# A hybrid decoder block on one core: the products that normalise x are pinned behind the second slot's logits

## The chip, the core and the metric

The kernel runs on one core of a Trainium2 chip. The metric is the device time of one execution in microseconds (us). The core has a matrix engine (TensorE, PE in the rows), three engines for elementwise work (VectorE or DVE, ScalarE or ACT, GpSimd or POOL) and a queue engine that issues DMAs (SyncE, SP). Each of them takes its own instructions one after another and waits, where needed, until another engine or a DMA has got far enough.

## The reference

One layer on 512 tokens of width 1024, float32 throughout:

```python
h = rms_norm(x, g_mix)
z = h @ w_in                     # q, k, v of mixers A and C, branch B, three gates
o_a = dilated window attention   # 12 heads in 3 groups (window, dilation): (128,1) (512,4) (2048,16);
                                 # head j of the groups ("slot j") is merged by softmax over their log-sum-exp
o_b = rg_lru_branch(...)         # conv, gated linear recurrence, GeLU gate
o_c = moba_attention(...)        # 8 heads, own block and one earlier block of 256 keys
x = x + (gt_0*(o_a @ p_a) + gt_1*(o_b @ p_b) + gt_2*(o_c @ p_c)) @ w_out
x = x + (silu(gate) * up) @ w_down       # [gate, up] = rms_norm(x, g_ffn) @ w_gu
return rms_norm(x, g_final)
```

## The kernel before, in words

**Products.** Every matrix product is taken as three products of split operands, hi*hi + hi*lo + lo*hi (`mm3`, lines 200 to 202). The weights come as 147 chunks of 128x1024, in the order of one list. For each chunk `stage` issues the DMA to `wraw` (three buffers), ScalarE casts it to `whi` (line 178) and VectorE or, for chunks 7 to 61, GpSimd subtracts to get `wlo` (line 183, four pieces of 256 columns). A `project` is 24 products with 512 columns each. Results go to the eight PSUM banks (`bank`), so a new product can have to wait for the readers of an old one.

**Two forms of x.** `X` is the split of x*g (`xhi`, `xlo`), without the normalisation; what is projected from it is multiplied by the row of 1/rms afterwards (`unscaled`, line 479: `qt`, `kt`, from `rq` and `rb`). `XN` is the split of x*g*rb. To make it the kernel loads x once more (`reload`, eight tiles `xt2`, shown as `xt` in the rows), multiplies (line 926, VectorE), casts `hi` (line 249, ScalarE) and subtracts to get `lo` (line 250, VectorE).

**Mixer A, slot by slot.** For slot j, `la(j)` gives three steps of logits: `s0` (line 562, `head_logits`), `s1` and `s2` (lines 579 and 585, `class_logits`: add the bias, then add and take the minimum into `m` or `stp`). `wa(j)` takes exponentials (line 594), adds their sums (line 710) and exchanges the statistics through DRAM, `exch` (lines 718 and 720), since groups are laid out by token or by residue class. `wa2(j)` computes the factors from `mm` (line 728) to `ff` and scales the probabilities (line 599). `ta(j)` transposes them on TensorE (lines 608 and 622, the flips) and splits them into `ph`, `pl` (lines 611, 612) and `pp` (lines 628, 629). `xa(j)` multiplies these with the values (lines 659 and 780).

**Order.** Code is written in the order of the list below, with some steps woven into a projection. The framework's scheduler then sets the order on each engine by its own estimate of times, not by the order in the code alone. `tc.keep_in_program_order` keeps an instruction behind everything that is written earlier for its engine. The stretch of interest, as written (`fa(h, i, w)` projects pair i of half h, w = 0 for q and 1 for k):

```python
reload(); d0, st = la(0)
for outs in weave(class_values_g(), 32, st, 12): VA.append(values_out(outs, True))
wa(d0); fa(0, 2, 0); fa(0, 2, 1); wa2(d0)
renorm(range(8))
d1, st = la(1)
VC.append(values_out(values_mm(st, 12)))
wa(d1); st = ta(d0)
VC.append(values_out(values_mm(st)))
fa(1, 0, 0); xa(d0); fa(1, 0, 1); wa2(d1); fa(1, 1, 0)   # and so on
```

Of the kernel before, what the change touches and what calls it, by code (L numbers as in the profile page):

```python
# [10 lines left out]
ALU = mybir.AluOpType  # L11
# [7 lines left out]
KT = 8  # L19
# [112 lines left out]
def layer_kernel(tc, x0p, xT, wts, tab, oneh, msk, idn, gfin, out):  # L132
    nc = tc.nc
# [3 lines left out]
    with (  # L137
# [10 lines left out]
        def uid(s):  # L148
            cnt[0] += 1
            return f"{s}_{cnt[0]}"  # L150
# [7 lines left out]
        def f32(ap):  # L158
            return ap.bitcast(F32)
# [69 lines left out]
        def project(act, kind="m", steps=(), first=0):  # L229
            return weave(project_g(act, kind), 8, steps, first)  # L230
# [36 lines left out]
        prm = cst.tile([128, 48], F32)  # L267
# [4 lines left out]
        for k in range(KT):  # L272
            if k == 0:
                xt = xp[:, 0:512]
            else:
                xt = tp.tile([128, 512], F32, name=uid("xt"), tag="bias")
                nc.sync.dma_start(xt, xT[k])
            for p in FIRST[k]:
# [7 lines left out]
                lo, in0=xt, scalar=g, in1=f32(hi), op0=ALU.mult, op1=ALU.subtract  # L286
# [305 lines left out]
        def expo(lay, negm, den):  # L592
            for qb in range(4):
                nc.scalar.activation(lay[qb][0], lay[qb][0], AF.Exp, scale=-1.0,
                                     bias=negm[:, qb : qb + 1], accum_out=den[:, qb : qb + 1])
# [22 lines left out]
        def flip_pairs(srcs):  # L618

            bt = bank()  # L620
            for i, p in enumerate(srcs):
                nc.tensor.transpose(bt[:, i * 128 : i * 128 + 128], p, ident)  # L622
            r = []
            for b in range(2):
                t = slot(F32R, "pp")
                t4 = t.rearrange("p (c two n) -> p c two n", two=2, n=128)
                src = bt[:, b * 256 : b * 256 + 256].rearrange("p (c n) -> p c n", c=2)
                nc.scalar.copy(t4[:, :, 0, :], src)
                nc.vector.tensor_sub(t4[:, :, 1, :], src, f32(t4[:, :, 0, :]))
                r.append(t)  # L630
            return r
# [36 lines left out]
        def ea(ps, half, i, w, scaled=False):  # L668
            pair = A_PAIRS[half][i]
            perm = [g > 0 for g, _ in pair]  # L670
            r = None if scaled else (rq, rb)[w]
            t = (q_tiles, k_tiles)[w](ps, r, perm)
            for n in range(2):
                qk[pair[n] + (w,)] = t[n]

        def fa(half, i, w, steps=(), first=0):
            scaled = half == 1
            ea(project(XN if scaled else X, "ma", steps, first), half, i, w, scaled)

        def st_part(st, s, o):  # L680

            c = o * 8 + s * 4
            return st[:, c : c + 4]
# [19 lines left out]
        def wa(d):  # L703

            stn, stp, j = d["stn"], d["stp"], d["j"]
            expo(d["lay"][0], st_part(stn, 0, 0), st_part(stn, 1, 0))
            dd = sm.tile([128, 8], F32, name=uid("dd"), tag="dd")
            for g in (1, 2):
                expo(d["lay"][g], st_part(stp, 0, 0), dd[:, g * 4 - 4 : g * 4])
            nc.vector.tensor_add(st_part(stp, 1, 0), dd[:, 0:4], dd[:, 4:8])  # L710
            a = exch[j : j + 1, :]

            def dram(n, by):
                ap = [[1, 128], [512, 2], [128, 4]] if by == 0 else [[4, 128], [512, 2], [1, 4]]
                return bass.AP(tensor=a.tensor, offset=a.offset + n * 1024, ap=ap)

            for n, st in enumerate((stn, stp)):
                nc.scalar.dma_start(dram(n, n), st[:, 0:8])
            for n, st in enumerate((stp, stn)):
                nc.sync.dma_start(st[:, 8:16], dram(n, 1 - n))  # L720
# [26 lines left out]
        def ta(d):  # L747
            j = d["j"]

            def vf(kt):  # L750
                return VA[0][kt][:, j * 128 : j * 128 + 128]

            d["m0"], steps = turn(d["lay"][0], vf, True)
            d["p"] = {}

            def cls(g):
                d["p"][g] = flip_pairs([p for p, _ in d["lay"][g]])

            return steps + [lambda g=g: cls(g) for g in (1, 2)]
# [155 lines left out]
        x_again = []  # L915
# [4 lines left out]
                nc.sync.dma_start(xt, xT[k])  # L920
                x_again.append(xt)

        def renorm(ks):
            for k in ks:
                xt = x_again[k]
                nc.vector.scalar_tensor_tensor(xt, in0=xt, scalar=prm[:, k : k + 1], in1=rb,
                                               op0=ALU.mult, op1=ALU.mult)
                XN.append(split(xt))

        zs = []  # L930
# [19 lines left out]
        rb = norm_all(dg)  # L950
# [10 lines left out]
        for outs in weave(class_values_g(), 32, st, 12):  # L961
# [2 lines left out]
        fa(0, 2, 0)  # L964
        fa(0, 2, 1)
        wa2(d0)
        renorm(range(8))
        d1, st = la(1)
        VC.append(values_out(values_mm(st, 12)))
        wa(d1)  # L970
        st = ta(d0)
        VC.append(values_out(values_mm(st)))
        fa(1, 0, 0)
# [27 lines left out]
                                op0=ALU.mult)  # L1001
# [83 lines left out]
        for m in range(8):  # L1085
# [7 lines left out]
            for b in (0, 2, 1):  # L1093
                ps = bank()
                nk = len(O[b])
                for k in range(nk):
# [6 lines left out]
                                               op0=ALU.add, op1=ALU.mult)  # L1103
# [12 lines left out]
        for m in range(8):  # L1116
            xr = tp.tile([128, 512], F32, name=uid("xr"), tag="bias")
            nc.sync.dma_start(xr, xT[m])
            if m == 0:
# [10 lines left out]
                                           op0=ALU.mult, op1=ALU.subtract)  # L1130
# [68 lines left out]
        for tb in range(4):  # L1199
# [4 lines left out]
            for c0, c1 in cuts:  # L1204
# [18 lines left out]
                if (c0, c1) != cuts[-1]:  # L1223
# [4 lines left out]
                                            op0=ALU.mult, op1=ALU.add)  # L1228
# [113 lines left out]
```

## Time and profile before

| what | value |
|---|---|
| median of 3 runs (lowest to highest) | 889.67 us (889.59 to 889.92) |
| the profiled execution, its span | 888.6 us, 886.6 us |
| TensorE, VectorE, ScalarE, GpSimd busy | 875.2, 472.8, 399.3, 283.9 us |
| granted TensorE clock over the span | 0.996 |

The span is the time from the first to the last instruction of the profiled execution; some 2 us lie around it. Times in the rows count from the start of the span. Shares of busy time tell how much an engine had to do, not whether anyone waited for it: that is read from the waits and from the order in time.

### The profile page before, as it was taken

Reading aid. Unit: us, or ns where it says so; the run is one execution under the profiler, and the core shown is the slowest. Engines: PE = TensorE matmul, PEld = TensorE weight load, DVE = VectorE, ACT = ScalarE, POOL = GpSimd, SP = SyncE. Lnnn points to the kernel's source line nnn. Section 1 sums busy time; section 2 is a strip of 40 time slices with the busy share of each in tenths; the row PEclk is TensorE's granted clock in tenths of the full one; section 3 lists DMA queues with packets and bytes.
Section 4 is the critical chain, followed back from the end, with each engine's and each line's share of the span. In section 5 each row is a group of like instructions: output and inputs, shape, how many; then the busy total and the mean of one; then the engine's idle time right before and its main releaser. Section 6 shows DMA issues by size and latency. Waiting matters only on the chain.

```text
span 886.6 us, 11269 instructions
## 1 busy us (share of the span) xinstructions
PE 875.2 (99%) x4166; PEld 737.4 (83%) x4166; DVE 472.8 (53%) x922; ACT 399.3 (45%) x692; POOL 283.9 (32%) x328
## 2 busy tenths in 40 slices
PE   9999999999999999999999999999999999999996
PEld 7897988888888888888888888888888888888885
DVE  7498947566665656647425445444444444322226
ACT  7376754664675567762323434333223332222213
POOL 2157364655543434675111312111222111000004
PEclk9999999999999999999999999999999999999999
DMA  7247332652322221232223322222222222222202
GB/s 276 93 158 111 94 127 88 108 133 96 95 95 84 84 95 47 97 119 95 95 95 119 119 92 84 88 94 95 95 95 99 100 103 104 96 95 95 95 24 96
DMA packets 40279, 90.28 MB, mean 102 GB/s; under 512 B 13988, under 2 KB 15780, under 8 KB 40224
## 3 DMA queue, kind: packets, MB, share of 16 engines
q1 hardware_dynamic: 34048, 88.26, 30.8%
q10 hardware_dynamic: 5824, 0.98, 0.7%
q8 instruction: 33, 0.54, 0.3%
q0 software_dynamic: 352, 0.33, 0.2%
q14 instruction: 22, 0.18, 0.1%
HBM read 87.34 MB, written 2.20 MB: 101 GB/s over the span
## 4 chain that ended last, share of the span: by engine, by line
PE 88%; DVE 4%; issue 3%; POOL 2%; DMA 2%; ACT 1%; DVEq 0%; POOLq 0%; ACTq 0%
PE ps L200 23%; PE ps L201 23%; PE ps L202 23%; PE ps L1189 12%; POOL wlo L183 2%; DMA wraw<-in_wts 2%; PE ps L659 2%; PE ps L608 1%; PE ps L555 1%; PE ps L554 1%; DVE y L1234 1%; DVE lo L250 0%; PE ps L622 0%; PE ps L780 0%; ACT junk L1220 0%
## 5 line engine op out<-in xcount | busy, mean ns | idle before, releaser
L178 ACT CAST whi<-wraw 128x1024 fp32r<-128x1024 f32 (+1 forms) x149 | 154.6, 1039 | 274.9 <-issue 101.5
L183 POOL TENSOR_TENSOR wlo<-wraw,whi 128x256 fp32r<-128x256 f32 x220 | 169.6, 803 | 181.1 <-ACT whi L178 181.0
L200 PE MATMUL ps<-hi,whi 128*128 128x512 f32 x520 | 205.2, 395 | 0.0
L201 PE MATMUL ps<-lo,whi 128*128 128x512 f32 x520 | 202.9, 390 | 0.0
L202 PE MATMUL ps<-hi,wlo 128*128 128x512 f32 x520 | 202.7, 390 | 0.0
L183 DVE TENSOR_TENSOR wlo<-wraw,whi 128x1024 fp32r<-128x1024 f32 (+1 forms) x94 | 117.5, 1250 | 115.5 <-ACT whi L178 115.5
L200 PE MATMUL ps<-uhi,whi 128*128 128x512 f32 x352 | 137.9, 392 | 0.0
L202 PE MATMUL ps<-uhi,wlo 128*128 128x512 f32 x352 | 137.1, 389 | 0.0
L201 PE MATMUL ps<-ulo,whi 128*128 128x512 f32 x352 | 136.9, 389 | 0.0
L202 PEld LDWEIGHTS ps<-hi,wlo 128*128 128x128 f32 x520 | 97.6, 188 | 20.6
L200 PEld LDWEIGHTS ps<-hi,whi 128*128 128x128 f32 x520 | 97.7, 188 | 18.8
L201 PEld LDWEIGHTS ps<-lo,whi 128*128 128x128 f32 x520 | 97.8, 188 | 18.5
L1163 POOL TENSOR_TENSOR av<-sg,uu 128x512 f32<-128x512 f32 x22 | 45.7, 2077 | 198.5 <-DVE sg L1161 198.5
L202 PEld LDWEIGHTS ps<-uhi,wlo 128*128 128x128 f32 x352 | 66.1, 188 | 14.0
L201 PEld LDWEIGHTS ps<-ulo,whi 128*128 128x128 f32 x352 | 66.1, 188 | 13.5
L200 PEld LDWEIGHTS ps<-uhi,whi 128*128 128x128 f32 x352 | 66.1, 188 | 13.3
L1189 PE MATMUL ps<-wlo,hi 128*128 128x512 f32 (+1 forms) x180 | 57.7, 384 | 0.0
L1189 PE MATMUL ps<-whi,lo 128*128 128x512 f32 (+1 forms) x180 | 57.7, 384 | 0.0
L1189 PE MATMUL ps<-whi,hi 128*128 128x512 f32 (+1 forms) x180 | 57.1, 384 | 0.0
L1159 DVE TENSOR_TENSOR uu<-ps,rb 128x512 f32<-128x512 f32 x22 | 15.2, 690 | 64.9 <-PE ps L202 64.9
L1222 POOL TENSOR_TENSOR y<-x,gf 128x512 f32<-128x512 f32 (+1 forms) x8 | 9.7, 1229 | 108.3 <-DVE x L1212 107.9
L200 PE MATMUL ps<-whi,xhi 128*128 128x256 f32 (+1 forms) x128 | 40.4, 318 | 0.3 <-DVE stn L562 0.3
(232 smaller groups left out, 1236.2 us busy)
## 6 DMA issues: line engine op xcount, KB each, us to landing
wraw<-in_wts SPq DMA_DIRECT2D x145, 512.0 KB, 3.2
xt<-in_xT SPq DMA_DIRECT2D x15, 256.0 KB, 5.5
bias<-relb SPq DMA_DIRECT2D x8, 256.0 KB, 6.9
xr<-in_xT SPq DMA_DIRECT2D x8, 256.0 KB, 2.7
out<-y SPq DMA_DIRECT2D x7, 256.0 KB, 2.4
wraw<-in_wts SPq DMA_DIRECT2D x4, 256.0 KB, 4.9
bias<-relb SPq DMA_DIRECT2D x4, 128.0 KB, 4.5
bias<-relb SPq DMA_DIRECT2D x8, 64.0 KB, 5.1
```

Source lines behind the costliest of these rows:

```text
L178: nc.scalar.copy(hi[:, cc], raw[:, cc])
L183: eng.tensor_sub(lo[:, dd], raw[:, dd], f32(hi[:, dd]))
L200: nc.tensor.matmul(o, lh, rh, start=start, stop=False)
L201: nc.tensor.matmul(o, lh, rl, start=False, stop=False)
L202: nc.tensor.matmul(o, ll, rh, start=False, stop=stop)
L554: nc.tensor.matmul(bk, qh[:, qc], kk[:, k0 : k0 + nn], start=True, stop=False)
L555: nc.tensor.matmul(bk, ql[:, qc], kk[:, k0 : k0 + nn], start=False, stop=True)
L659: nc.tensor.matmul(po[:, o0 : o0 + n], vf(kt), p, start=(i == 0), stop=(i == len(mms) - 1))
L1159: nc.vector.tensor_mul(uu, pu, r2)
L1163: nc.gpsimd.tensor_mul(av, sg, uu)
L1189: nc.tensor.matmul((acc[tb][hf] if o is None else o)[:, cc], l[:, t], r[:, hf * 512 + cc.start : hf * 512 + cc.stop], start=((k == 0 or fi ...
L1222: eng.tensor_mul(y2[hf][:, cc], x, gf[hf][:, cc])
```

## The change

The eight products of `renorm` are written after the second slot's logits and exponentials (`wa(d1)`) instead of after `wa2(d0)`, and each is pinned behind what is written before it for VectorE. The splits follow in a loop of their own. The projections of pair 0 of half 1, `fa(1, 0, 0)` and `fa(1, 0, 1)`, use `X` instead of `XN`; their results pass through `unscaled`.

```diff
         def fa(half, i, w, steps=(), first=0):
-            scaled = half == 1
+            scaled = (half, i) > (1, 0)
             ea(project(XN if scaled else X, "ma", steps, first), half, i, w, scaled)
...
-        def renorm(ks):
-            for k in ks:
+        def renorm():
+            for k in range(KT):
                 xt = x_again[k]
-                nc.vector.scalar_tensor_tensor(xt, in0=xt, scalar=prm[:, k : k + 1], in1=rb,
-                                               op0=ALU.mult, op1=ALU.mult)
+
+                tc.keep_in_program_order(nc.vector.scalar_tensor_tensor(
+                    xt, in0=xt, scalar=prm[:, k : k + 1], in1=rb, op0=ALU.mult, op1=ALU.mult))
+            for xt in x_again:
                 XN.append(split(xt))
...
         wa2(d0)
-        renorm(range(8))
         d1, st = la(1)
         VC.append(values_out(values_mm(st, 12)))
         wa(d1)
+        renorm()
         st = ta(d0)
         VC.append(values_out(values_mm(st)))
         fa(1, 0, 0)
```

In the changed file the products stand in line 927, and line numbers behind them are two higher.

VectorE, at the first slot's logits, in the kernel before (`stn` and `m` are results of the logits, `P` their tiles, `xt` the tiles of x):

```order
L562 ISA stn_586 128x1
L926 SCALAR_TENSOR_TENSOR xt_120_576<-xt_120_576,prm,rb_410 128x512
L926 SCALAR_TENSOR_TENSOR xt_121_578<-xt_121_578,prm,rb_410 128x512
L579 TENSOR_TENSOR P_706<-ps_707,bias_704 128x256
L579 TENSOR_TENSOR P_706<-ps_713,bias_704 128x256
L926 SCALAR_TENSOR_TENSOR xt_122_580<-xt_122_580,prm,rb_410 128x512
L926 SCALAR_TENSOR_TENSOR xt_123_582<-xt_123_582,prm,rb_410 128x512
L926 SCALAR_TENSOR_TENSOR xt_124_584<-xt_124_584,prm,rb_410 128x512
L585 ISA P_706,m_127_588<-ps_707,P_706 128x128
```

The same place in the changed kernel:

```order
L562 ISA stn_586 128x1
L579 TENSOR_TENSOR P_706<-ps_707,bias_704 128x256
L579 TENSOR_TENSOR P_706<-ps_713,bias_704 128x256
L585 ISA P_706,m_127_588<-ps_707,P_706 128x128
L585 ISA m_127_588 128x1
```

The five products between the logits are gone from here, and so are three that stood ahead of line 562.

VectorE, ahead of the flips of slot 0, in the kernel before (`lo` is the low part of XN, `pl` and `pp` the split probabilities):

```order
L599 TENSOR_SCALAR P_706<-P_706,ff_941 128x128 x4
L599 TENSOR_SCALAR P_745<-P_745,ff_941 128x128 x4
L710 TENSOR_TENSOR stp_992<-dd_1174 128x4
L455 SCALAR_TENSOR_TENSOR v_1167<-ps_1061,mixr_361,v_1167 128x4x64
L612 TENSOR_TENSOR pl_1234<-ps_1228,ph_1233 128x512
L612 TENSOR_TENSOR pl_1260<-ps_1255,ph_1259 128x384
L629 TENSOR_TENSOR pp_1292<-ps_1287,pp_1292 128x2x128
L629 TENSOR_TENSOR pp_1295<-ps_1287,pp_1295 128x2x128
```

The same place in the changed kernel:

```order
L927 SCALAR_TENSOR_TENSOR xt_123_582<-xt_123_582,prm,rb_410 128x512
L927 SCALAR_TENSOR_TENSOR xt_124_584<-xt_124_584,prm,rb_410 128x512
L250 TENSOR_TENSOR lo_1157<-xt_117_570,hi_1156 128x512
L250 TENSOR_TENSOR lo_1161<-xt_118_572,hi_1160 128x512
L250 TENSOR_TENSOR lo_1165<-xt_119_574,hi_1164 128x512
L250 TENSOR_TENSOR lo_1169<-xt_120_576,hi_1168 128x512
L250 TENSOR_TENSOR lo_1173<-xt_121_578,hi_1172 128x512
L250 TENSOR_TENSOR lo_1177<-xt_122_580,hi_1176 128x512
L250 TENSOR_TENSOR lo_1181<-xt_123_582,hi_1180 128x512
L250 TENSOR_TENSOR lo_1185<-xt_124_584,hi_1184 128x512
L612 TENSOR_TENSOR pl_1234<-ps_1228,ph_1233 128x512
L612 TENSOR_TENSOR pl_1260<-ps_1255,ph_1259 128x384
```

All eight products (six more stand above these rows, behind line 710) and all eight `lo` now stand between line 710 and the first `pl`. Before, the `lo` stood between the steps of `wa2(d0)`; the scalings of line 599 now stand among the second slot's logits, ahead of the last four of line 585.

ScalarE, at the same place, in the kernel before (`ph`, `pp` from the flips, `whi` a weight chunk):

```order
L611 CAST ph_1233<-ps_1228 128x512
L718 DMA exch<-stp_992 128x2x4
L611 CAST ph_1259<-ps_1255 128x384
L628 CAST pp_1292<-ps_1287 128x2x128
L628 CAST pp_1295<-ps_1287 128x2x128
L628 CAST pp_1321<-ps_1316 128x2x128
```

In the changed kernel:

```order
L249 CAST hi_1184<-xt_124_584 128x512
L178 CAST whi_1358<-wraw_1357 128x1024
L611 CAST ph_1233<-ps_1228 128x512
L178 CAST whi_1436<-wraw_1435 128x1024
L611 CAST ph_1259<-ps_1255 128x384
L628 CAST pp_1292<-ps_1287 128x2x128
```

The eight casts of `hi` (the last of them is shown) and two weight casts now stand ahead of the casts of the flips.

## Rows read from the trace of the kernel before

**Rows 1.** The page: busy us, share of the span, instructions of each engine.
```profile
PE 875.2 (99%) x4166; PEld 737.4 (83%) x4166; DVE 472.8 (53%) x922; ACT 399.3 (45%) x692; POOL 283.9 (32%) x328
```

**Rows 2.** The waits of TensorE: us in total, times, longest.
```profile
PE ps L200 <- DVE m L585: 2.2, 1, 2.2
```

**Rows 3.** Timeline of TensorE: start, us, instruction [idle before and releaser].
```profile
70.80 0.39 PE L201 MATMUL ps<-wlo,xhi 128*128 128x512 f32 x1
71.03 0.40 PE L202 MATMUL ps<-whi,xlo 128*128 128x512 f32 x1
73.63 0.47 PE L200 MATMUL ps<-xhi,whi 128*128 128x512 f32 x1 [2.20 <-DVE m L585]
...
74.87 0.63 PE L202 MATMUL ps<-xhi,wlo 128*128 128x512 f32 x1
...
78.28 0.39 PE L201 MATMUL ps<-xlo,whi 128*128 128x512 f32 x1
```

**Rows 4.** Busy time by stretch: PE, PEld, DVE, ACT, POOL, clock, DMA, GB/s.
```profile
74.80:77.90 3.10, 3.10 (x9) 2.38 (x9) 2.37 (x12) 3.03 (x14) 0.00 (x0) 0.51 0.45 24
```

**Rows 5.** Timeline of VectorE at the first slot's logits.
```profile
63.27 3.14 DVE L926 SCALAR_TENSOR_TENSOR xt<-xt,prm,rb 128x512 f32<-128x512 f32 x3 [0.32 <-DMA xt<-in_xT]
...
70.05 3.01 DVE L926 SCALAR_TENSOR_TENSOR xt<-xt,prm,rb 128x512 f32<-128x512 f32 x3
72.99 0.28 DVE L585 CUSTOM_DVE_ANT_0 P<-ps,P 128x128 f32<-128x128 f32 x1
```

**Rows 6.** Timeline of ScalarE at the first slot's exponentials.
```profile
63.38 1.28 ACT L594 ACT_TABLE_LOAD   x1
66.65 0.40 ACT L594 ACTIVATE P<-P,stn 128x128 f32<-128x128 f32 x1 [1.98 <-DVE stn L562]
```

**Rows 7.** The chain that ended last, 60 to 125 us: start, us, what.
```profile
70.09 11.59 DMA wraw<-in_wts
...
87.24 0.70 DVE kt L479
...
92.97 0.16 DVE mm L728
```

**Rows 8.** DMA issues from 56 to 84 us: count, KB, us to landing.
```profile
exch<-stn ACTq DMA_DIRECT2D x1, 4.0 KB, 9.6
```

**Rows 9.** Timeline of VectorE: the flips of slot 0, then a later `mm`.
```profile
109.31 0.15 DVE L710 TENSOR_TENSOR stp<-dd 128x4 f32<-128x4 f32 x1
...
109.78 1.19 DVE L612 TENSOR_TENSOR pl<-ps,ph 128x512 fp32r<-128x512 f32 x2
...
111.74 0.76 DVE L629 TENSOR_TENSOR pp<-ps,pp 128x256 fp32r<-128x256 f32 x2 [0.44 <-ACT pp L628]
...
137.73 0.15 DVE L728 TENSOR_TENSOR mm<-stp 128x4 f32<-128x4 f32 x1
...
139.24 3.85 DVE L599 TENSOR_SCALAR P<-P,ff 128x128 f32<-128x128 f32 x8
```

**Rows 10.** Instructions by form, ScalarE, 104 to 108 us: count | busy, mean ns.
```profile
L594 ACT ACTIVATE P<-P,stp 128x128 f32<-128x128 f32 x8 | 3.1, 400 | 0.0
```

**Rows 11.** Timeline of TensorE at the products of slot 0.
```profile
119.07 0.28 PE L659 MATMUL ps<-ph,v 128*128 128x256 f32 x1
...
120.02 1.12 PE L780 MATMUL ps<-pp,v 128*128 128x256 f32 x8
```

**Rows 12.** Lines 926 and 250 alone: ns lowest/median/highest, first and last start.
```profile
L926 DVE SCALAR_TENSOR_TENSOR xt<-xt,prm,rb x8: 737/1214/1228, 63.3 to 71.9; 128x512 f32<-128x512 f32 x8
...
L250 DVE TENSOR_TENSOR lo<-xt,hi x8: 659/684/685, 93.1 to 98.8; 128x512 fp32r<-128x512 f32 x8
```

**Rows 13.** By form, GpSimd, 62 to 74 us, then 102 to 109.
```profile
L183 POOL TENSOR_TENSOR wlo<-wraw,whi 128x256 fp32r<-128x256 f32 x12 | 12.0, 1030 | 8.4 <-ACT whi L178 8.4
...
L183 POOL TENSOR_TENSOR wlo<-wraw,whi 128x256 fp32r<-128x256 f32 x8 | 5.6, 747 | 11.3 <-ACT whi L178 11.3
```

**Rows 14.** Busy time from 120 to 130 us, columns as in rows 4.
```profile
120.00:130.00 10.00, 10.00 (x50) 8.46 (x49) 5.11 (x8) 6.59 (x12) 7.63 (x12) 1.00 0.29 106
```

## The prediction

> **What bounds the kernel now.** I read the busy shares first: TensorE is busy for 875.2 of the 886.6 us of the span [rows 1], so a change can only be worth what TensorE waits for, or what new waiting it causes. TensorE's waits come second, and the longest one after the start is a single wait of 2.2 us, put down to VectorE's logits of line 585 [rows 2]. The timeline of TensorE shows where it lies: the last product of the class values starts at 71.03 us, the next one (the first of `fa(0,2,0)`) at 73.63, with 2.20 us idle [rows 3]. A second loss follows it. From 74.87 to 78.28 us eight products are started, 0.426 us each, where the neighbours come every 0.23 us (70.80 to 71.03), and in that stretch the granted clock is 0.51, the lower of its two levels, 1.2 of 2.4 GHz [rows 3, 4]. That is 3.41 - 8 x 0.23 = 1.6 us. Together the place costs 3.8 us.
>
> VectorE's timeline says why. The eight products `xt2*g*rb` of line 926 stand ahead of and between the first slot's logits: three from 63.27 us (3.14 us), three more from 70.05 (3.01 us), and the logits of line 585 that free TensorE's bank follow at 72.99 [rows 5]. Nobody waits for these products at that time.
>
> **The change, part by part.**
>
> *The stall at 71 us goes.* Without the eight products line 562 can begin when VectorE is free, near 63 us instead of 66.3. Two products of the class logits and the four sums of line 585 then end near 66 us, 5 us before TensorE asks for the bank. The weights of `fa(0,2,0)` are no new bound: in the trace they were in place for the start at 73.63, and the two chunks are split by GpSimd from 62.1 to 70.1 us, now without the eight products beside them. So TensorE gains 2.2 + 1.6 = 3.8 us here, and would reach the products of slot 0 (line 659) at 119.07 - 3.8 = 115.3 us [rows 11].
>
> *The same eight products now stand on VectorE between the second slot's logits and the flips of slot 0.* That is the term that decides. Behind them stand the eight `lo` of line 250, then `pl` and `pp` (lines 612 and 629), and TensorE's products of lines 659 and 780 need exactly those. In the trace `pl` starts at 109.78 us and the second `pp` ends at 111.74 + 0.38 = 112.1 [rows 9], while TensorE's second product of line 780, its reader, starts at 120.02 + 0.12 = 120.14 [rows 11]. The slack is 8.0 us. What the change does to VectorE's side, step by step:
>
> a) Start of the stretch, the `mm` of line 728, now at 92.97 us [rows 7]. Its chain goes back over `kt` (87.24) to a weight chunk issued at 70.09 and 11.59 us on its way [rows 7], while the write of `stn` to DRAM, in runs of 4 bytes and 9.6 us long [rows 8], fills the same DMA engines. ScalarE's exponentials, which start that write, waited for line 562 until 66.65; now they wait for the table load that ends at 63.38 + 1.28 = 64.7 [rows 6]. So write, chunk and chain come 1.9 us earlier, and `mm` starts at 91.1. The bounds are 0 (the transfers are no earlier) and 4.3 us (the chunk no longer matters and `kt` follows TensorE's own 3.8 us).
>
> b) From `mm` to the sum of line 710 it took 109.31 - 92.97 = 16.3 us [rows 7, 9]. The eight `lo` leave it, 8 x 0.61 = 4.9 us (0.68 each [rows 12], 0.07 of it overlapped with the next): 11.4 us remain. But these covered waits that now show. The chain from `mm` to the first scaling takes 1.51 us when nothing stands between its steps (137.73 to 139.24 [rows 9]), some 0.6 of it work, so 0.9 us, and 0.3 for the second one. And line 710 waits for ScalarE's eight exponentials of the class groups (3.1 us [rows 10]), which can't start before the last logits; these now stand behind the eight scalings, so some 2.0 us of them are bare. 11.4 + 1.2 + 2.0 = 14.6: line 710 at 105.7.
>
> c) One `v` (0.4) and the eight products. The eight rows run from 0.737 to 1.228 us, with a median of 1.214 [rows 12]; while they ran, GpSimd's subtractions took 1.03 us each, against 0.75 from 102 to 109 us [rows 13]. GpSimd's two chunks of that time are 5.6 us of work [rows 13] whose casts come some 3 us earlier with the change, since ScalarE no longer casts `hi` ahead of them; I estimate them done by 105, with nothing to do until the `hi` are cast. So I take the shortest row, 8 x 0.74 = 5.9 (bound: 8 x 1.0 = 8.0, the pace at 63 and 70 us [rows 5]): 112.0.
>
> d) The eight `lo`, 4.9 us. Half of them meet GpSimd's next chunk, whose cast stands right behind the `hi` on ScalarE; I add 1.0 us (bounds 0 and 2.5, by the two rates of c): 117.9. The Trainium skill (SBUF — State Buffer, section "SBUF: two separate sides") says that a VectorE instruction with two SBUF inputs and a GpSimd instruction that reads SBUF exclude each other for a whole instruction. By it the four subtractions would be added in full, 4 x 0.75 = 3.0 us, and the forecast would be 2.0 us higher; the trace is milder, since a full exclusion would make 0.74 + 0.75 = 1.49 us of each product and the median was 1.21.
>
> e) From `pl` to the end of the second `pp`: 112.1 - 109.78 = 2.3 us, as now: 120.2. TensorE's second product of line 780 then starts at 120.3 instead of 120.14.
>
> So TensorE, there at 115.3, is held by `pl`, `pl`, `pp` and `pp` in turn until 120.3, with ten products of 0.12 us between. It comes out 0.15 us behind the kernel before. The 3.8 us are given back, and the low clock that followed a 2.2 us gap is likely to follow this one of nearly 4 us too: I take the same 1.6 us (bounds 0 and twice that).
>
> *The projection pair that uses `x*g`.* Same number of products on TensorE. VectorE gets a `qt` and a `kt` more, 0.7 us each [rows 7], near 122 to 130 us, where it is busy for 5.11 of 10 us [rows 14]; this idle time hides them. The unscaled pair is what lets TensorE go on without XN until about 126 us; with XN ready at 117.9, XN itself holds nobody.
>
> Sum: +0.15 + 1.6 = +1.75 us. The profiled execution took 888.6 us, its span 886.6; with the change 890.3. The median of the runs lies 1.07 us above that execution (889.67), so 891.4.
>
> **The rivals.**
>
> *The slack is enough (faster).* If the chunk of step a lands so early that `kt` only follows TensorE, `mm` starts 4.3 us earlier, at 88.7, and the second `pp` ends at 117.8. TensorE then comes out 2.3 us ahead, with 0 to 1.6 us of clock lost: 889.67 - 2.3 = 887.4. For it: the chunk's 11.59 us is the longest landing in that stretch and could shrink, and products without GpSimd beside them are cheap. Against it: the write of `stn` that slows the chunk is still issued before it.
>
> *VectorE is later still (slower).* If GpSimd's subtractions slide into the eight products, these cost 8.0 instead of 5.9, and the `lo` 1.5 more; ScalarE besides has two weight casts between `hi`, the first `ph` and the second, and one of them waits for a chunk issued behind another `exch` transfer. With 2 to 3 us of that: 889.67 + 1.75 + 2.6 = 894.0. It decides from the point at which line 710 comes after 107 us. For it: eight rows of before, of which most are at 1.2 us. Against it: GpSimd's timing above. The skill's rule of step d, a full exclusion, is the strong form of this case: it alone would bring the time to 893.4.
>
> *The stall only moves.* If another wait (a weight chunk, a bank) takes the gap's place near 71 to 82 us and the slack of the flips holds, the time stays at 889.7.
>
> **How the numbers follow.** Forecast (VectorE becomes the bound at the products of slot 0) 0.50, faster rival 0.22, slower rival 0.23, moved stall 0.05. The forecast's own range is 889.3 to 893.2 (clock loss 0 to 3.2 with the other terms fixed, and a little of step a). For 8 in 10 I take 887.0 to 894.0. About 0.2% (1.8 us) can be told from no change here: below 887.9 is faster, above 891.4 slower. The forecast lies at that edge, so it gives half of its chance to the one side and half to the other, less a little; with the rivals: faster 0.20, within 0.38, slower 0.42.
>
> **What would show it.** Right: no idle time of TensorE at 71 us and full clock from 71 to 82; line 710's second sum near 106 us; the eight products of `renorm` right behind it at 0.7 to 0.8 us each; TensorE idle near 115 to 120 us at lines 659 and 780, released by `pl` and `pp`, and a stretch at the lower clock behind it. Wrong: if TensorE passes line 659 without waiting, the forecast is wrong and the kernel is faster by 2 us or more; if the wait there is over 6 us, step c or d was undersized; if TensorE is idle between 78 and 110 us, a cause that I have not named took the gain.

## The result, and the profile of the changed kernel

The changed kernel takes 899.74 us (median of 4 runs, 899.05 to 901.15) where the kernel before takes 889.63 (889.46 to 889.92): ratio 1.0117, 95% interval [1.0104, 1.0130], so 10.1 us slower. The forecast was 891.4, with a range up to 894.0: too low. The profiled execution took 899.05 us, its span 897.3. In the traces of e1, e2, e5, e6, e7, e8, e10 and e12 the granted clock is low between 30 and 42 us (0.80 from 30 to 36 us in e6, 1.00 in the kernel before), so that the table load of line 594 starts 1.4 to 1.9 us later than the 63.38 us of [rows 6], and every later time with it; this late start is taken off below where the text says so.

First the waits of TensorE from 60 to 170 us, which answer to [rows 2]; a row names what waits, what released it, the sum, the number and the longest:

```profile
PE ps L622 <- DVE P L599: 4.0, 2, 3.5
PE ps L554 <- DVE kk L524: 3.4, 1, 3.4
PE ps L608 <- DVE P L599: 1.1, 3, 0.5
PE ps L659 <- ACT ph L611: 0.6, 1, 0.6
PE ps L659 <- DVE pl L612: 0.2, 1, 0.2
```

The 2.2 us for line 585 are gone. Two waits stand in their place that the kernel before did not have: `kk` of the second slot's logits (line 554), and the scaled `P` at the flips of that slot (lines 608 and 622). Its timeline says where (start, us, instruction, idle before it and the releaser; here and below rows are left out where the start times jump):

```profile
81.88 0.28 PE L200 MATMUL ps<-whi,xhi 128*128 128x256 f32 x1
91.58 0.36 PE L554 MATMUL ps<-kk,qh 128*128 128x256 f32 x1 [3.43 <-DVE kk L524]
92.13 0.41 PE L554 MATMUL ps<-kk,qh 128*128 128x256 f32 x1
95.54 0.28 PE L200 MATMUL ps<-whi,xhi 128*128 128x256 f32 x1
119.04 0.28 PE L659 MATMUL ps<-ph,v 128*128 128x256 f32 x1
120.05 0.38 PE L659 MATMUL ps<-ph,v 128*128 128x256 f32 x1 [0.62 <-ACT ph L611]
151.09 1.07 PE L622 MATMUL ps<-ident,P 128*128 128x128 f32 x2 [3.50 <-DVE P L599]
162.26 0.28 PE L554 MATMUL ps<-kk,qh 128*128 128x256 f32 x1
```

The same places in the kernel before, TensorE again (the product that starts at 81.88 us above, slot 1's first logits, its last flips, slot 2's first logits; line 659 is in [rows 11]):

```profile
86.24 0.28 PE L200 MATMUL ps<-whi,xhi 128*128 128x256 f32 x1
92.35 0.28 PE L554 MATMUL ps<-kk,qh 128*128 128x256 f32 x1
142.21 0.60 PE L622 MATMUL ps<-ident,P 128*128 128x128 f32 x4
151.30 0.28 PE L554 MATMUL ps<-kk,qh 128*128 128x256 f32 x1
```

Read side by side: at 82 us TensorE is 86.24 - 81.88 = 4.36 us ahead. At line 659 it stands where it stood before (119.04; 119.07 in [rows 11]): the lead is lost between 88 and 96 us, 3.43 us of idle time and 16 products at 0.213 instead of 0.12 us (92.13 to 95.54). At slot 2's first logits it is 162.26 - 151.30 = 10.96 us behind. So by line 659 the gain is given back, and the 10 us come from 119 to 162. The busy time by stretch (PE, PEld, DVE, ACT, POOL, granted clock, DMA, GB/s) shows the clock with it:

```profile
70.00:80.00 10.00, 10.00 (x45) 8.42 (x45) 2.40 (x6) 4.30 (x15) 3.81 (x6) 1.00 0.94 73
90.00:100.00 10.00, 8.42 (x58) 8.45 (x59) 8.73 (x36) 5.38 (x16) 2.03 (x3) 0.83 0.25 88
140.00:150.00 10.00, 6.43 (x29) 4.47 (x27) 8.60 (x25) 4.92 (x11) 3.87 (x6) 1.00 0.26 93
150.00:160.00 10.00, 8.27 (x29) 6.37 (x30) 7.02 (x17) 2.58 (x8) 2.52 (x6) 0.66 0.15 52
```

**The wait at 88 us.** `kk` hangs on the chain of slot 1's `q` and `k` tiles, and that on ScalarE and SP. A piece of the chain that ended last, a chunk issued beside it (KB, us to landing), and the timelines of ScalarE and of SP:

```profile
66.50 15.12 DMA exch<-stn
```

```profile
wraw<-in_wts SPq DMA_DIRECT2D x1, 512.0 KB, 15.1
```

```profile
82.19 1.20 ACT L454 ACTIVATE v<-ps,mixr 128x256 fp32r<-128x256 f32 x3 [7.89 <-DMA exch<-stn]
```

```profile
81.69 0.37 SPq L720 DMA_DIRECT2D stp<-exch  x1
82.67 0.37 SPq L177 DMA_DIRECT2D wraw<-in_wts  x1
```

The write of `stn` is issued 2.15 us earlier than before and takes 15.12 us instead of 9.6 [rows 8]; it lands at 81.6 instead of 78.3. ScalarE stands at its second write for 7.89 us with the `v`, `qh` and `kk` casts queued behind it, and SP at the read of `exch` with a weight chunk behind it. The chunk that SP issued at 67.59 us, beside the write, is as long on its way (15.1 us).

How much of this TensorE can bear stands in the kernel before, and the working did not ask for it: the `kk` of line 524 ended there at 88.62 + 1.09 = 89.71 us, and TensorE asked at 92.35. The slack was 2.6 us, less than the 4.36 us of the lead.

```profile
88.62 1.09 DVE L524 TENSOR_TENSOR kk<-kt,kk 64x512 fp32r<-64x512 f32 x1 [0.69 <-ACT kk L523]
```

**The wait at 145 us.** VectorE from slot 1's `mm` on; these rows answer to [rows 7, 9]:

```profile
94.39 0.16 DVE L728 TENSOR_TENSOR mm<-stn 128x4 f32<-128x4 f32 x1
107.65 0.16 DVE L710 TENSOR_TENSOR stp<-dd 128x4 f32<-128x4 f32 x1 [2.11 <-ACT P L594]
107.73 4.06 DVE L927 SCALAR_TENSOR_TENSOR xt<-xt,prm,rb 128x512 f32<-128x512 f32 x6
113.42 4.89 DVE L250 TENSOR_TENSOR lo<-xt,hi 128x512 fp32r<-128x512 f32 x8
118.24 0.68 DVE L612 TENSOR_TENSOR pl<-ps,ph 128x512 fp32r<-128x512 f32 x1
122.85 0.42 DVE L629 TENSOR_TENSOR pp<-ps,pp 128x256 fp32r<-128x256 f32 x1 [0.74 <-ACT pp L628]
137.23 3.65 DVE L519 TENSOR_TENSOR kk<-kt,kk 64x256 fp32r<-64x256 f32 x4 [0.30 <-ACT kk L517]
140.92 0.17 DVE L728 TENSOR_TENSOR mm<-stn 128x4 f32<-128x4 f32 x1
150.24 3.20 DVE L599 TENSOR_SCALAR P<-P,ff 128x128 f32<-128x128 f32 x8
```

`mm` of slot 1 starts at 140.92, 8.3 us later than in the kernel before:

```profile
132.60 0.16 DVE L728 TENSOR_TENSOR mm<-stn 128x4 f32<-128x4 f32 x1
```

Its last scalings end at 153.4. In the kernel before they ended at 139.24 + 3.85 = 143.1 [rows 9] and TensorE took the last flips of line 622 at 143.34: a slack of about 0.25 us. The scalings are 10.3 us later where `mm` is 8.3 later: from the `mm` for `stp` to the last eight scalings it takes 3.39 us (146.85 to 150.24) where it took 1.51 (137.73 to 139.24 [rows 9]), since three `kk` of the next pair now stand between. In the kernel before they stood behind the scalings. VectorE had idle time on the way there, in which it could do nothing: from 131.3 us it waited for ScalarE's `hp`, which stood behind a weight cast that waited for GpSimd (VectorE, then ScalarE):

```profile
135.39 0.68 DVE L784 TENSOR_TENSOR hp<-ps,hp 64x512 f32<-64x512 f32 x1 [4.14 <-ACT hp L783]
```

```profile
133.82 1.06 ACT L178 CAST whi<-wraw 128x1024 fp32r<-128x1024 f32 x1 [3.40 <-POOL wlo L183]
```

This is read from the trace; no run tests it by itself.

### The profile page after: what moved, and what is told of

Same layout as the page of the kernel before. It is cut to its first block, busy times and chain, and to the rows that moved or that the text cites. A ratio compares the mean times of both kernels' runs of the same rounds, so it can differ in the third digit from the quotient of the medians.

```text
span 897.3 us, 11271 instructions
## 1 busy us (share of the span) xinstructions
PE 878.9 (98%) x4166; PEld 739.6 (82%) x4166; DVE 473.0 (53%) x924; ACT 402.0 (45%) x692; POOL 283.6 (32%) x328
## 4 chain that ended last, share of the span: by engine, by line
PE 86%; DVE 7%; ACT 3%; DMA 2%; issue 1%; POOL 0%; ACTq 0%; DVEq 0%; SPq 0%
PE ps L200 23%; PE ps L201 22%; PE ps L202 22%; PE ps L1191 12%; DMA exch<-stn 2%; DVE kk L519 2%; PE ps L659 2%; PE ps L608 1%; DVE P L599 1%; PE ps L555 1%; PE ps L554 1%; DMA wraw<-in_wts 1%; ACT whi L178 1%; ACT P L594 1%; DVE qq L469 1%
## 5 line engine op out<-in xcount | busy, mean ns | idle before, releaser
L200 PE MATMUL ps<-hi,whi 128*128 128x512 f32 x504 | 199.6, 397 | 0.0
L201 PE MATMUL ps<-lo,whi 128*128 128x512 f32 x504 | 197.4, 392 | 0.0
L202 PE MATMUL ps<-hi,wlo 128*128 128x512 f32 x504 | 197.2, 391 | 0.0
L202 PEld LDWEIGHTS ps<-hi,wlo 128*128 128x128 f32 x504 | 95.1, 189 | 20.4
L200 PEld LDWEIGHTS ps<-hi,whi 128*128 128x128 f32 x504 | 95.2, 189 | 18.5
L201 PEld LDWEIGHTS ps<-lo,whi 128*128 128x128 f32 x504 | 95.2, 189 | 18.2
L201 PEld LDWEIGHTS ps<-ulo,whi 128*128 128x128 f32 x352 | 66.1, 188 | 13.5
L200 PEld LDWEIGHTS ps<-uhi,whi 128*128 128x128 f32 x352 | 66.1, 188 | 13.3
```

Source lines behind the costliest of these rows:

```text
L200: nc.tensor.matmul(o, lh, rh, start=start, stop=False)
L201: nc.tensor.matmul(o, lh, rl, start=False, stop=False)
L202: nc.tensor.matmul(o, ll, rh, start=False, stop=stop)
```

## The experiments

Ratios are to the kernel before on the same chip, with 95% intervals; the edit is against the kernel that the row names.

| run | edit | us | ratio |
|---|---|---|---|
| e1 | changed kernel, normalised x for the pair | 898.03 | 1.0096 [1.0077, 1.0115] |
| e2 | kernel before, x*g for the pair | 893.22 | 1.0047 [1.0032, 1.0062] |
| e3 | changed, two DRAM tensors | 901.24 | 1.0135 [1.0114, 1.0157] |
| e4 | changed, `wa2(d1)` earlier | 900.48 | 1.0134 [1.0116, 1.0152] |
| e5 | products behind `wa(d0)`, normalised x | 892.63 | 1.0045 [1.0027, 1.0063] |
| e6 | changed, 32-byte write | 893.44 | 1.0052 [1.0036, 1.0068] |
| e7 | e5 and the 32-byte write | 889.97 | 1.0007 [0.9997, 1.0017] |
| e8 | kernel before, 32-byte write | 889.48 | 1.0001 [0.9992, 1.0011] |
| e9 | e7, `lo` behind slot 1's logits | 884.66 | 0.9959 [0.9946, 0.9971] |
| e10 | e9, x*g for the pair | 891.02 | 1.0023 [1.0014, 1.0032] |
| e11 | changed, one DMA more | 900.47 | 1.0126 [1.0111, 1.0142] |
| e12 | e9 with the 4-byte write | 889.94 | 1.0009 [1.0000, 1.0019] |

**e1 and e2: the two halves apart.** e1 takes the first line out of the change, e2 puts it alone into the kernel before:

```diff
-            scaled = (half, i) > (1, 0)
+            scaled = half == 1
```

> Only the first half of the change: the eight products are pinned behind the second slot's logits, and fa(1,0,0) and fa(1,0,1) use the normalised x as in the kernel before. Theory P (the x*g pair is what makes the second slot late: its q and k tiles need an extra product and longer casts ahead of the pinned mm of slot 1): TensorE idles some 6 us at 113.6 to 120, where it now has nothing to do while it waits for ph, pl and the normalised x, but lines 608 and 622 of the second slot then wait less than 1 us; time 893 to 896. Theory R (VectorE's 9 us lateness at slot 0's pp, from the moved products, makes slot 1 late whatever the pair reads): the same 6 us at 113.6, and still over 2 us of waiting at lines 608 and 622; time 897 to 901. The stall at 88 us (3.4 us, line 554) is there by both.

> Only the second half of the change on the kernel before: fa(1,0,0) and fa(1,0,1) read x*g; the eight products stay where they were, ahead of the first slot's logits. Theory P: mm of slot 1 goes from 132.6 us to 137 or later, lines 608 and 622 of slot 1 wait 3 us or more, time 893 to 896. Theory R: the pair costs about 1 us on VectorE's and ScalarE's chain, mm of slot 1 at 133 to 134.5, no wait of 1 us at lines 608 and 622, time 889.4 to 890.8. The stall at 71 us stays by both.

Each half alone is slower, so neither theory stands alone. In e1 lines 608 and 622 still wait 4.9 us (theory R, at 898.0), with 1.7 us at `lo` in place of the 6 expected. In e2 the time, 893.2, is at the lower edge of theory P, with the wait at 71 us still there. `mm` of slot 1 starts at 136.03, 134.4 with the late start taken off, and TensorE waits 1.7 us for the scalings at line 622: both lie between the two theories. Measured from TensorE's first product of line 659 (120.39 here, 119.07 before), `mm` is 15.64 instead of 13.53 us behind, so the pair made it 2.1 us later, not the 3.4 that the clock of the traces shows and that the expectation of e10 uses. Where the pair's price lies, VectorE in e2 (the first `kk`; then all four, ns from shortest over median to longest; then `mm`), and the kernel before:

```profile
130.90 2.93 DVE L519 TENSOR_TENSOR kk<-kt,kk 64x256 fp32r<-64x256 f32 x1 [0.28 <-ACT kk L517]
```

```profile
L519 DVE TENSOR_TENSOR kk<-kt,kk x4: 600/765/2931, 130.9 to 135.4; 64x256 fp32r<-64x256 f32 x4
```

```profile
136.03 0.16 DVE L728 TENSOR_TENSOR mm<-stn 128x4 f32<-128x4 f32 x1
```

```profile
130.02 0.87 DVE L519 TENSOR_TENSOR kk<-ps,kk 64x256 fp32r<-64x256 f32 x2 [0.81 <-ACT kk L517]
```

With x*g the tile goes through `kt` in SBUF, and the `kk` read two SBUF tiles. The 1.28 us each that the expectation of e10 names is a mean of 2.93, 0.92, 0.61 and 0.60: one `kk` took 2.93 us while GpSimd ran its subtractions, the others 0.6 to 0.9. From PSUM it was 0.44 each before.

**e3 and e11: what ScalarE waits for.** e3 gives the two exchanged tiles a DRAM tensor each; e11 leaves the tensor and issues one small DMA more between the two writes. Of e3's edit the first lines are shown; the others change the addresses (...).

```diff
-        exch = dr.tile([4, 4 * 512], F32)
+        exch = [dr.tile([4, 2 * 512], F32, name=uid("exch")) for _ in range(2)]
...
```

> The changed kernel with one edit: the two exchanged tiles go through two DRAM tensors, so that ScalarE's write of stp no longer stands behind the landing of stn's write. Theory S (ScalarE, blocked for 7.9 us until that landing at 81.6 us, made kk of line 524 late): ScalarE's idle stretch at 74 to 82 us goes, qt comes near 77 instead of 83.9 us, TensorE's wait of 3.43 us at line 554 falls to 0 to 2.2 us (2.2 if ScalarE then stands at a weight cast whose chunk SP issues behind the same landing); time 895 to 898.5. Theory D (the DMA queue of SP decides, which waits for that landing too, so that the chunk comes at 87.5 us and ScalarE's kk behind it): the wait at line 554 stays at 2 us or more and the time at 898.5 to 900.

```diff
             a = exch[j : j + 1, :]
+            if j == 0:
+                spare = sm.tile([128, 4], F32, name=uid("spare"), tag="spare")
+                nc.sync.dma_start(spare, stp[:, 0:4])
```

> The changed kernel with one 16-byte-a-row DMA more on SP (a copy of stp's first columns into an unused tile, issued after the first write). DMAs wait on semaphores DMAHW0 to 7 in turn; in the changed kernel both DRAM writes of ScalarE have number 7, so that the second waits for the first to land, and in the kernel before it waits for another DMA, done long ago. With the extra DMA the second write has number 0 again. Theory Q (the shared semaphore is what blocks ScalarE): ScalarE issues the second write by 75.5 us in place of 81.7, its idle 7.9 us go, qt starts near 77 in place of 83.9 us; SP still waits for the landing before its next weight chunk, so line 554 waits 1.5 to 2.6 us in place of 3.43, ratio 1.008 to 1.012. Rival: ScalarE is idle until 81 us all the same, the wait stays at 3 us or more.

e3 changed nothing at ScalarE: it is idle for 6.57 us until the landing, line 554 waits 2.4 us, the time is not better. Its wait is on a DMA semaphore (number 7, which both writes have), not on the tensor. e11 gave the second write another number, and it waited all the same:

```profile
80.42 0.38 ACTq L721 DMA_DIRECT2D exch<-stp  x1
80.85 1.20 ACT L454 ACTIVATE v<-ps,mixr 128x256 fp32r<-128x256 f32 x3 [6.34 <-DMA bias<-relb]
```

```profile
bias<-relb SPq DMA_DIRECT2D x1, 64.0 KB, 13.5
```

The DMA it now waits for, a bias tile, is issued at 66.9 us and lands at 80.3, when the wait ends: 13.5 us after its issue. So theory Q is out: with another semaphore ScalarE waits for another DMA, issued beside the write, and that one is as late.

**e6 and e8: the write itself.** `stn` is written as it lies, in 128 runs of 32 bytes, and the two reads of `stp` do the permutation (`flat`, defined ahead of these lines, is an address in the same tile of DRAM):

```diff
...
-            for n, st in enumerate((stn, stp)):
-                nc.scalar.dma_start(dram(n, n), st[:, 0:8])
-            for n, st in enumerate((stp, stn)):
-                nc.sync.dma_start(st[:, 8:16], dram(n, 1 - n))
+            nc.scalar.dma_start(flat(0, [[8, 128], [1, 8]]), stn[:, 0:8])
+            nc.scalar.dma_start(dram(1, 1), stp[:, 0:8])
+            for s in range(2):
+                nc.sync.dma_start(stp[:, 8 + 4 * s : 12 + 4 * s], flat(4 * s, [[1, 4], [32, 32], [8, 4]]))
+            nc.sync.dma_start(stn[:, 8:16], dram(1, 0))
```

> The changed kernel, with stn written to DRAM in runs of 32 bytes (128 of them) in place of 4 (1024), and the permutation done by the two reads of stp, in runs of 4 bytes. Theory W (the 4-byte write is what lands late, 15.1 us after its issue, and holds ScalarE and SP): the write lands in under 7 us, ScalarE's idle stretch before the second write is under 1.5 us in place of 7.9, SP issues the next weight chunk by 76 us in place of 82.7, the wait at line 554 is under 0.5 us and the clock stays full at 90 to 96 us; the waits at lines 608 and 622 stay over 2 us: ratio to the kernel before 1.005 to 1.009. Rival D (the DMA engines are full at 66 to 80 us, whatever the run length): the write still takes over 10 us, the wait at line 554 stays over 2 us, ratio 1.010 to 1.014.

> The kernel before with only the 32-byte write of stn, as a control: in it line 554 does not wait for kk, so an earlier landing is worth nothing to TensorE: ratio 0.998 to 1.002, the stall at 71 us as before. If the ratio is below 0.997, the write had a price in the kernel before too, which its trace did not show at TensorE.

W is right. Issued at 68.17, the write has landed by 73.04, when SP's read behind it goes out: under 4.9 us. ScalarE does not stand still, and SP's chunk leaves at 75.10; ScalarE and SP in e6:

```profile
64.87 1.28 ACT L594 ACT_TABLE_LOAD   x1
68.17 0.33 ACTq L720 DMA_DIRECT2D exch<-stn  x1
73.83 0.39 ACTq L721 DMA_DIRECT2D exch<-stp  x1
```

```profile
73.04 1.95 SPq L723 DMA_DIRECT2D stp<-exch  x2
75.10 1.06 SPq L177 DMA_DIRECT2D wraw<-in_wts  x1
```

Line 554 does not wait, the clock is full from 70 to 140 us, and TensorE reaches line 659 at 115.58 us without a wait: 3.5 us ahead of the kernel before by the clock of the traces, 5.0 us with the late start of 1.5 us taken off (the prediction had 3.8). What is left, 4.0 and 1.1 us at lines 622 and 608 as in the changed kernel, is the second cause: ratio 1.0052 with the lead kept, so that it costs more than these 5 per mille. In the kernel before the same edit is worth nothing (e8, 1.0001): there `kk` came 2.6 us before TensorE asked for it. Why the write lands 5.5 us later in the changed kernel (15.12 instead of 9.6) no run isolates; the DMA share around it was 0.94.

**e4: only the order of `mm`.**

```diff
         xa(d0)
-        fa(1, 0, 1)
         wa2(d1)
+        fa(1, 0, 1)
```

> The changed kernel with one line moved: wa2(d1), and with it the pinned mm of slot 1, stands ahead of fa(1,0,1) in the program. Theory O (the data of slot 1's mm are there long before 140.9 us, and it is only its place behind the k tiles of the x*g pair that makes it late): mm at 136 us, first scaling near 140 instead of 144.8, TensorE's waits at lines 608 and 622 fall from 5.1 to 1.5 us or less and the low clock at 150 to 157 us with them; time 892 to 894.5. Rival T (the transfer of stn or ScalarE's exponential holds it at the same time): time 898.5 to 900.

Theory O failed. `mm` came at 136.06 us, as expected, but the next step that VectorE has to do (`wd`) stands behind the pair's `kk` and a `qq`:

```profile
138.43 3.26 DVE L519 TENSOR_TENSOR kk<-kt,kk 64x256 fp32r<-64x256 f32 x4
141.72 0.68 DVE L471 SCALAR_TENSOR_TENSOR qq<-ps,qq 64x512 fp32r<-64x512 f32 x1
142.43 0.17 DVE L736 TENSOR_TENSOR wd<-ee,stn 128x8 f32<-128x8 f32 x1
```

The first scaling starts at 143.96, 0.85 us earlier than in the changed kernel, but the last ends 1.7 us later (155.2), and lines 608 and 622 wait 6.5 us in all. A chain in an in-order queue is as late as its last link.

**e5 and e7: the products into VectorE's idle stretch.** In the changed kernel VectorE does nothing from 74.8 to 82.7 us; e5 puts the products there and lets the pair read the normalised x (as in e1), e7 adds the 32-byte write.

```diff
         wa(d0)
+        renorm()
         fa(0, 2, 0)
         fa(0, 2, 1)
         wa2(d0)
+        for xt in x_again:
+            XN.append(split(xt))
...
         wa(d1)
-        renorm()
```

> The eight products are pinned right behind wa(d0), in the stretch of 74 to 82 us in which VectorE is idle in the changed kernel, and fa(1,0,0) and fa(1,0,1) use the normalised x as in the kernel before. Theory V (what made the second slot late was that VectorE came 9 us later to the pp of slot 0, because products and lo stood ahead of them): slot 0's pp end near 114 us as before, lines 608 and 622 of slot 1 wait under 0.5 us, the stall at 71 us is gone. With theory W (the write of stn lands late whenever the 71 us stall is gone, and ScalarE and SP stand behind it) line 554 still waits 2 to 3.5 us and the clock falls behind it, so the two cancel: ratio to the kernel before 0.999 to 1.002. Without W the whole 3.8 us are gained: ratio 0.995 to 0.997. If V is wrong: waits over 2 us at lines 608 and 622, ratio over 1.004.

> The two edits of the runs before this together: the eight products right behind wa(d0), the normalised x for fa(1,0,*), and stn written in runs of 32 bytes. By V and W no wait is left at 71, 88 and 145 us: TensorE gains the 3.8 us of the first stall, ratio to the kernel before 0.994 to 0.997 (884.5 to 887). By rival D or if V is wrong: 0.999 or more.

V's sign came: neither run waits at lines 608 and 622, though slot 0's last `pp` starts at 117.9 and 115.7 us, not near 114 as expected. The distance to TensorE fits that: this `pp` starts 5.3 us ahead of TensorE's first product of line 659 in both runs, as in the kernel before (113.76 and 119.07), and 3.8 us behind it in the changed kernel (122.85 and 119.04). But TensorE was held up ahead of it here, so these two runs alone do not prove V; e9 below, where TensorE keeps its lead, does more. Neither run gains. The place that took it is new: TensorE in e5, and then in e7, waits for the second slot's logits on VectorE:

```profile
PE ps L200 <- DVE stn L562: 4.0, 1, 4.0
```

```profile
PE ps L200 <- DVE stn L562: 3.3, 1, 3.3
```

The eight `lo` (5 us) stand ahead of line 562 here, as in the kernel before, where TensorE came later, by 2 us (e5) to 4 us (e7) with the late start taken off, and waited 0.3. The stall of 71 us had moved to 100 us.

**e9, e10 and e12: `lo` behind the second slot's logits.** e9 pins them where the change pins the products (`split` gets an argument `pin` for it); e10 adds the pair on x*g, e12 takes the 32-byte write back out.

```diff
-        for xt in x_again:
-            XN.append(split(xt))
...
         wa(d1)
+        for xt in x_again:
+            XN.append(split(xt, pin=True))
```

> The run e7 (products right behind wa(d0), normalised x for fa(1,0,*), stn written in runs of 32 bytes) with the eight lo of line 250 (251 is their pair) pinned behind the second slot's logits, where the change puts the products. Theory: e7 gave its gain back because the eight lo, 5 us on VectorE, stood ahead of the second slot's logits (TensorE waited 3.31 us for line 562 there). Behind them only the lo are left on VectorE, not products and lo, so that slot 0's pp and slot 1's mm are not late for TensorE: waits under 1 us in all from 60 to 170 us, ratio 0.994 to 0.997. Rival: the lo alone already make TensorE wait for the normalised x at 110 us or for slot 1's scalings at 140 us, over 2 us: ratio 0.999 or more.

> The run e9 with x*g for fa(1,0,0) and fa(1,0,1), as in the change. By the price that e2 showed for the pair alone (mm of slot 1 later by 3.4 us, the four kk of line 519 at 1.28 us each from SBUF in place of 0.44 from PSUM), lines 608 and 622 of slot 1 wait 1 to 4 us more than in e9: ratio to the kernel before 0.998 to 1.003, at least 0.002 above e9's. If the pair costs only the extra qt and kt, as the prediction had it: same ratio as e9 within 0.001.

> The run e9 without its 32-byte write: products right behind wa(d0), lo pinned behind the second slot's logits, normalised x for fa(1,0,*), and stn written in runs of 4 bytes as before. If the write's landing is a cause of its own: line 554 waits 1 to 2.5 us (e5 had 1.24), the clock falls behind it when the wait is over 2 us, ratio to the kernel before 0.997 to 1.002, at least 0.002 above e9's 0.9959. If the order on VectorE was all that counted: the same ratio as e9 within 0.0015.

e9 is the fastest: 884.66 us, 4.1 per mille (3.6 us) under the kernel before, about the 3.8 us of the stall. Its waits of TensorE from 60 to 170 us are these (lines 624 and 578 there are 622 and 576 here), with the clock full from 60 to 170:

```profile
PE ps L624 <- DVE P L601: 1.1, 1, 1.1
PE ps L578 <- DVE v L457: 0.5, 1, 0.5
```

Together the 1.6 us are more than the "under 1 us in all" expected. e10 shows the pair's price when all else is right: 891.02 us and ratio 1.0023, inside the range given, 6.4 us more than e9 by the medians and 5.7 by the ratios. Lines 624 and 601 wait 3.5 us instead of 1.1:

```profile
PE ps L624 <- DVE P L601: 3.5, 3, 2.8
```

with the granted clock at 0.66 from 140 to 150 us. e12 shows the write's price: line 556 (554 here) waits 1.2 us again, there are small waits at lines 661 and 782 (659 and 780 here), and the whole gain is gone (1.0009). So the slot 1 wait comes down in steps as its causes go: 5.1 us in e6, 3.5 in e10 with the products moved, 1.1 in e9 with the pair on the normalised x too.

## Why the prediction was wrong, step by step

- *The stall at 71 us goes: 3.8 us.* Right: no wait there, full clock from 70 to 80 us, 4.36 us of lead at 82 us.
- *Step a, "write, chunk and chain come 1.9 us earlier".* Wrong, and outside its bounds. The write went out 2.15 us earlier but landed 3.4 us later, and `mm` came at 94.39 instead of 91.1. The working took the transfer as a fixed 9.6 us, and did not ask who stands behind it: ScalarE and SP did, for 8 us. It looked for the price at slot 0 alone; the first place that asks for this chain is line 554, with 2.6 us of slack in the kernel before. Against a lead of 4.36 us even a chain as late as before would have made TensorE wait there for 1.7 us. This took the lead at 88 to 96 us, which the prediction named as the sign of "a cause that I have not named". e6, with e8 as its control, shows the write as the cause, 6.5 per mille (1.0117 against 1.0052).
- *Step b, 14.6 us from `mm` to line 710.* It took 107.65 - 94.39 = 13.3; 1.3 too much.
- *Step c, one `v` and eight products, 6.3 us.* 5.8 us (107.73 to 113.50), 0.68 us from one product to the next: right.
- *Step d, eight `lo`, 4.9 us and 1.0 for GpSimd.* 4.89 us: the 4.9 was right, the 1.0 not needed. GpSimd's four subtractions beside them took the loss instead:

```profile
115.19 5.81 POOL L183 TENSOR_TENSOR wlo<-wraw,whi 128x256 fp32r<-128x256 f32 x4 [8.21 <-ACT whi L178]
```

  1.45 us each, where they take 0.75 alone. By the Trainium skill (SBUF — State Buffer, section "SBUF: two separate sides") a VectorE instruction with two SBUF inputs and a GpSimd instruction that reads SBUF exclude each other. The trace fits that, 0.75 + 0.68 = 1.43 us, but GpSimd alone was the loser: the `lo` are no longer than before. In e2 it was VectorE, once: one `kk`, 64x256, took 2.93 us while GpSimd's four subtractions beside it kept their 0.75 or so each; the sixteen of that form in the kernel before have a median of 0.62.
- *Step e, 2.3 us from `pl` to the second `pp`.* 3.5 us (118.24 to 121.78), because `ph` stood behind a weight cast whose chunk landed late, as the slower rival had it.
- *Sum at slot 0.* TensorE reached line 659 with no lead instead of 3.8 us, so it waited little there (0.8 us), and the clock stayed full. It leaves slot 0 with two of eight products of line 780 done at 122.12; with the six that follow, 0.12 us each, it is 1.9 us behind the 120.98 of before. The prediction said 1.75, by another way: luck, from two errors that cancel (the lead was already lost, and the hold at slot 0 was shorter).
- *The pair on x*g, "this idle time hides them".* Wrong. It counted a `qt` and a `kt`, 1.4 us, against an idle share of half. But the idle time is waiting inside a chain that ends in a pinned `mm`; the reads that moved from PSUM to SBUF cost as much again (the four `kk` took 5.1 us in e2 and 3.65 in the changed kernel, 0.44 each from PSUM before); and TensorE needs that chain's end with 0.25 us of slack, which [rows 9] and TensorE's flips at 142 us would have told. e2 prices the pair at 4.7 per mille (4.2 us), e10 against e9 at 6.4 us. In the changed kernel itself it is worth less, and less surely: e1, without it, has 1.0096 against 1.0117, with intervals that overlap.
- *The end of the sum.* This is the step that failed by most, with step a beside it. The prediction stopped at slot 0's `pp` and put everything behind it, the pair included, at nothing. VectorE left that `pp` 9 us late (122.85 for 113.76), and slot 1's scalings, with 0.25 us of slack, came 10.3 us late. TensorE was 1.9 us behind at slot 0 and 10.96 us at slot 2's first logits: 9.1 us were lost where the sum has no term. e1, without the pair, still waits 4.9 us there; e9, with only the `lo` ahead of `pp`, the wide write and no pair, 1.1 us. Prices of the causes (write, products and `lo` ahead of `pp`, pair) overlap and do not add up. Idle time (3.6 and 1.7 us from 140 to 160) and the lower clock (0.66 from 150 to 160: 8.27 x 0.34 = 2.8 us) make 8.1 of the 9.1 us lost from 122 to 162; the rest I put, without a run for it, down to flips that come one at a time.
- *The rivals.* "VectorE later still" had the right sign and engine, and the wrong place: it priced 2.6 us at slot 0, and the loss was at slot 1. Its condition came (line 710 at 107.65 us, after 107), but by a late `mm` and not by GpSimd in the products, which took 0.74 us each. "The stall only moves" had the right kind for the wait at 88 us, and booked no loss for it.

## What to carry to other kernels

A lead won in one place is worth only what the next in-order queue allows: follow it through the next two or three places at which TensorE asks for something, and write down the slack at each, before it is booked as gain. Idle share of an engine hides nothing in a chain whose end is wanted at once. A slow transfer that costs nothing now may be hidden by the very stall that is to be removed; here three repairs were needed together (products early, `lo` late, wide write), neither pair of them that was run gave anything (e7, e12), and the projection pair had to stay on the normalised x (e10).

## What the hardware showed that I had not expected

- A 4 KB write to DRAM in 1024 runs of 4 bytes took 15.12 us to land among other traffic, and DMAs issued beside it were as late: a weight chunk of 512 KB 15.1 us (the changed kernel), a bias tile of 64 KB 13.5 us (e11). The same bytes in 128 runs of 32 took under 4.9 us (e6).
- VectorE's subtraction with two SBUF inputs, 64x256, has a median of 0.62 us in the kernel before, and beside a busy GpSimd took up to 1.06 us in the changed kernel and in e4 and once 2.93 in e2; with one input in PSUM, in the kernel before, 0.44.
- A wait of TensorE does not always cost the clock too. The same wait of 2.2 us at line 585 went with a granted clock of 0.83 from 70 to 80 us in the kernel before (part of the time at 1.2 instead of 2.4 GHz) and 1.00 in e2 and e8. At line 554 the mean from 90 to 100 us was 0.83 behind 3.4 us (the changed kernel) and 2.4 us (e3), and 1.00 with 2.3 us (e1), 1.7 us (e11) and 1.2 us (e5). But 1.7 us at `lo` went with 0.83 from 110 to 120 us in e1. So the length of the wait does not divide the cases, the 2 us that the expectation of e12 names included.
